# The neighbourhood attention's relative bias: loaded in the layout of its use instead of built with shift products

## The chip, the cores and the metric

The kernel runs on one core of one Trainium2 chip. Five engines work side by side, each through its own list of instructions in order: TensorE (PE, with its weight loads as PEld), VectorE (DVE), ScalarE (ACT), GpSimd (POOL) and SyncE (SP). SP and ACT also issue the DMA transfers; a DMA instruction stands in the engine's list like any other, so what follows it waits until it is issued. The metric is the time of one execution on the device in microseconds (us), as the median of several runs.

## The reference, cut to what matters

The program is two network blocks of two layers each over 256 tokens of width 1024, in float32: recurrent and block attention with a dense and a mixed-of-experts feed-forward network, then a second block on a latent stream x and a context stream. The part that changes is the neighbourhood attention in the second block. Its 256 queries are 4 grid rows of 64 columns, it has 8 heads of width 64, and a query sees the 16 columns around its own in all 4 rows, plus 256 context keys, under one softmax. A learned bias is added to the latent scores, by the distance in rows and in columns:

```python
in_win = (col[None, :] >= cs[:, None]) & (col[None, :] < cs[:, None] + kw)
dc_idx = jnp.clip(col[None, :] - col[:, None], -(kw - 1), kw - 1) + (NA_WIN_COLS - 1)
rpb_cols = rpb.astype(jnp.float32)[:, :, dc_idx]
...
    dr_idx = rs + jnp.arange(kh) - r + (NA_WIN_ROWS - 1)
    bias = jnp.take(rpb_cols, dr_idx, axis=1)
    bias = jnp.where(in_win[None, None], bias, NEG_INF)
    bias = bias.transpose(0, 2, 1, 3).reshape(h, GRID_W, kh * GRID_W)
    s_lat = jnp.einsum('bqhd,bkhd->bhqk', q_row, k_band).astype(jnp.float32) * scale + bias
```

The table `rpb` has 8 heads x 15 row distances x 31 column distances.

## The kernel before, in words

Every large product is made of weight tiles of 128 x 1024 floats. `wload` (line 295) loads one from memory into a raw tile `wraw` on SP's queue (line 305), splits it into a high part `whi` on ACT (line 246, two pieces) and a low part `wlo` on DVE (line 249, two pieces), and TensorE then multiplies high x high, low x high and high x low (line 261). There are six raw tiles and four tiles each for `whi` and `wlo`, so a load waits for an older tile's split and a split for an older tile's products.

The program is written as Python generators that are interleaved: `x_chain` carries the latent stream, and `ctx_rest` the feed-forward network of the context stream, whose work is put between the latent stream's steps at rates from the table `SIDE` (line 1993). `hT1` is the context stream's normalised input, `hid` its hidden layer, `cffy` its output, `cv` its convolution and `th` its gate. A scheduler then fixes one order for each engine. `x_chain` and `ctx_rest` start when the mixture of experts is done, behind a branch (line 1277) that all engines cross: first the layer normalisation `layer_norm` (line 426, result `h`) with its two rows `ln_g` and `ln_b` loaded on ACT's queue (line 423), then `modulated` (line 1376), which scales `h` into `xscr` and transposes it on TensorE (line 281).

`even_x` (line 1759) is the latent stream's mixer: the projections, the recurrent heads `mlstm`, their output stage `mlstm_out` (line 1709, working on `ktok`, transposed on TensorE into `yxh` and `yxl`), and then the attention. Between these two it builds the bias in two tiles `bias0` and `bias1` of 128 queries x 8 heads x 256 keys. It loads constants `consts_n` (a shift matrix and the window mask) and the table `rpb` with four DMAs (line 1775), each of 31 partitions x 8 heads x 4 floats, that is 248 pieces of 16 bytes. For each of the 64 key columns a product with a shifted slice of the matrix (line 1781) puts the right column distance on each query partition; each product is 64 x 64. It has two instructions on TensorE, so there are 128. After every eight columns VectorE adds the mask and writes the two bias tiles (line 1785, 16 additions). `attend` (line 1461) then adds the bias to the scores (line 1802, tile `S`). The loads depend on nothing computed, so the scheduler has put them right behind the branch, ahead of the first weight splits on ACT.

Of the kernel before, what the change touches and what calls it, by code (L numbers as in the profile page):

```python
# [12 lines left out]
ALU = mybir.AluOpType  # L13
# [3 lines left out]
P = 128  # L17
# [7 lines left out]
NEG = -1e30  # L25
# [33 lines left out]
def shape_consts():  # L59

    i = np.arange(P)
    parts = []

    def add(name, m):
        m = np.asarray(m, np.float32)
        parts.append((name, m))

    r, c = i[:, None], i[None, :]
    same64 = (r // 64) == (c // 64)
    add("ident", np.eye(P))  # L70
    add("ones", np.ones((P, P)))
    add("tri_incl", r <= c)
    add("tri_rev", r >= c)
    add("tri_strict", r < c)
    add("bd_incl", same64 & (r <= c))

    s, t = r % 64, np.arange(64)[None, :]
    add("h_strict", s < t)
    add("h_incl", s <= t)
    add("h_ident", s == t)  # L80
    add("lv0T", ((s // 2) == (t // 2)) & (s < t))
    for lv in range(1, 6):
        b = 2 ** lv
        add(f"lv{lv}", ((s // (2 * b)) == (t // (2 * b))) & ((s // b) % 2 == 1) & ((t // b) % 2 == 0))
    add("up", np.where(c > r, NEG, 0.0))
    add("lo", np.where(c < r, NEG, 0.0))
    add("last", np.broadcast_to(r == P - 1, (P, P)))
    add("first", np.broadcast_to(r == 0, (P, P)))
    e = np.zeros((P, 30))
    e[:64, 14] = 1  # L90
    e[64:, 15] = 1
    add("head_e", e)
    add("iota", np.broadcast_to(c, (P, P)))
    k8 = np.arange(8)
    add("lt8", np.broadcast_to((k8[None, :] < k8[:, None]).reshape(1, 64), (P, 64)))
    col = np.arange(64)
    cs = np.clip(col - 8, 0, 48)
    win = (col[None] >= cs[:, None]) & (col[None] < cs[:, None] + 16)
    add("win", np.tile(np.where(win, 0.0, NEG), (2, 1)))
    sh = np.zeros((P, 191))  # L100
    for rr in range(2):
        for dl in range(31):
            sh[rr * 32 + dl, 78 - dl + 64 * rr] = 1
    add("shift", sh)
    pos = np.arange(T)
    half = 8
    inv = np.float32(10000.0) ** (-np.arange(half, dtype=np.float32) / np.float32(half))
    cos = np.zeros((P, T), np.float32)
    sin = np.zeros((P, T), np.float32)
    rot = np.zeros((P, 32), np.float32)  # L110
    for j in range(32):
        src = (pos // 64) if j < 16 else (pos % 64)
        ang = src.astype(np.float32) * inv[j % 8]
        for base in (0, 64):
            cos[base + j] = np.cos(ang)
            sin[base + j] = np.sin(ang)
            if j % 16 < 8:
                rot[base + j + 8, j] = -1.0
            else:
                rot[base + j - 8, j] = 1.0  # L120
    add("cos", cos)
    add("sin", sin)
    add("rot", rot)
    groups = {"consts_w": ("bd_incl", "h_strict", "h_incl", "h_ident", "lv0T", "lv1", "lv2", "lv3", "lv4", "lv5"),
              "consts_n": ("win", "shift"), "consts_m": ("cos", "sin")}
    groups["ident"] = ("ident",)
    special = {n for g in groups.values() for n in g}
    groups["consts"] = tuple(n for n, _ in parts if n not in special)
    arrs, offs = {}, {}
    by = dict(parts)  # L130
    for g, names in groups.items():
        offs[g] = {}
        o = 0
        for n in names:
            offs[g][n] = (o, by[n].shape[1])
            o += by[n].shape[1]
        arrs[g] = np.ascontiguousarray(np.concatenate([by[n] for n in names], 1))
    return arrs, offs


def pack(inputs):

    out = {}
    cols = []
    for n, k in VEC_SPECS:
        v = np.asarray(inputs[n], np.float32).reshape(k, P)
        cols.append(v.T)
    out["vecs"] = np.ascontiguousarray(np.concatenate(cols, 1))
    for n in RAW:
        out[n] = np.ascontiguousarray(np.asarray(inputs[n]))  # L150
    out["rpb"] = np.ascontiguousarray(np.asarray(inputs["ev_rpb_2"])[0].transpose(2, 0, 1))
    out.update(shape_consts()[0])
    return out


def bc(ap, axis, n):
    u = ap.unsqueeze(axis)
    shp = list(u.shape)
    shp[axis] = n
    return u.to_broadcast(shp)  # L160
# [1187 lines left out]
def small(N, name):  # L1348
    return N.tp.tile([P, 512], F32, name=name, tag="hT", bufs=4)
# [359 lines left out]
def mlstm_out(N, st, ch, E, o):  # L1709

    nc = N.nc
    hs = E["kh"][:, 1024:2048]
    og = E["qo"][:, 1024:2048]
    g = N.row_load(N.a["ev_ml_norm_g_2"][0])
    N.tt(hs, hs, og, ALU.mult)
    h3 = hs.rearrange("p (n x) -> p n x", n=8)
    mu = N.sm(8, "mu")
    nc.vector.tensor_reduce(mu, h3, axis=AX.X, op=ALU.add)
    N.ts(mu, mu, 1.0 / 128)
    N.tt(h3, h3, bc(mu, 2, 128), ALU.subtract)  # L1720
    N.act(og, hs, AF.Square)
    vr = N.sm(8, "vr")
    nc.vector.tensor_reduce(vr, og.rearrange("p (n x) -> p n x", n=8), axis=AX.X, op=ALU.add)
    rs = N.sm(8, "rs")
    N.rpow(rs, vr, 8, 1.0 / 128, 1e-6)
    N.tt(h3, h3, bc(rs, 2, 128), ALU.mult)
    h2 = hs.rearrange("p (b x) -> p b x", b=2)
    N.tt(h2, h2, bc(g[:, :512], 1, 2), ALU.mult)
    for k in range(0, 4, 2):
        p = N.ps(ch)  # L1730
        for i in range(2):
            for tb in range(2):
                N.tr(p[:, i * T + tb * P:i * T + (tb + 1) * P], h2[:, tb, (k + i) * P:(k + i + 1) * P])
        N.split(o.h[:, (4 + k) * T:(6 + k) * T], o.l[:, (4 + k) * T:(6 + k) * T], p)
# [24 lines left out]
def even_x(N, st, ch, x, S):  # L1759
    nc, a, c = N.nc, N.a, N.c  # L1760
    yield from even_proj(N, st, ch, x, S, "Ex")
    E, Ec = st["Ex"], st["Ec"]
    yield from paced(mlstm(N, st, ch, E, st["CT"], st["ms"], True), SIDE["mlstm"])
    o = N.act_slots(S["h"][0], S["h"][1], "yx")
    mlstm_out(N, st, ch, E, o)
    N.load_consts("consts_n", small(N, "consts_n"))

    bias = [N.slot(S["b"][i], f"bias{i}") for i in range(2)]
    rp = small(N, "rpb")
    nc.gpsimd.memset(rp[:, 0:64], 0.0)  # L1770
    r4 = rp[:, 0:64].rearrange("p (t h j) -> p t h j", t=2, h=8)
    for rr in range(2):
        for jt in range(2):
            s = 7 - 2 * jt - rr
            nc.scalar.dma_start(r4[rr * 32:rr * 32 + 31, jt], a["rpb"][:, :, s:s + 4])

    sh = c["shift"]
    for c0 in range(0, 64, 8):
        p = N.ps(ch)
        for i in range(8):  # L1780
            N.mm(p[:, i * 64:(i + 1) * 64], sh[:64, 63 - c0 - i:191 - c0 - i], rp[:64, 0:64], True, True)
        for jt in range(2):
            src = p.rearrange("p (c t x) -> p t x c", c=8, t=2)[:, jt]
            dst = bias[jt].rearrange("p (x c) -> p x c", c=64)[:, :, c0:c0 + 8]
            N.tt(dst, src, bc(c["win"][:, c0:c0 + 8], 1, 32), ALU.add)
        yield SIDE["bias"]
    qo, kv, kvc = E["qo"], E["kv"], Ec["kv"]

    def score(pr, hh, qt, p):
        q = slice(hh * 64, hh * 64 + 64)  # L1790
        l = qo[q, pr * T + qt * P:pr * T + (qt + 1) * P]
        N.mm(p[:, 0:T], l, kv[q, pr * T:(pr + 1) * T], True, True)
        N.mm(p[:, T:2 * T], l, kvc[q, pr * T:(pr + 1) * T], True, True)

    def vsrc(pr, hh, b):
        t = kv if b < 2 else kvc
        o_ = 1024 + (b % 2) * 512 + (2 * pr + hh) * 64
        return t[:, o_:o_ + 64]

    def biased(pr, hh, qt, p, S_):  # L1800
        h = 2 * pr + hh
        N.stt(S_[:, 0:T], p[:, 0:T], 0.125, bias[qt][:, h * T:(h + 1) * T], ALU.mult, ALU.add)
        N.act(S_[:, T:2 * T], p[:, T:2 * T], AF.Copy, scale=0.125)
    yield from paced(attend(N, ch, o, 4, 4, score, vsrc, 0.125, biased, ch2=1 - ch), SIDE["na"])
    st["yx_act"] = o
# [187 lines left out]
SIDE = dict(moba_in=0, moba=1, moba_out=0, start=5, mlstm=1.25, bias=0.5, na=0.5, res0=3, end0=5, mla=1.5)  # L1993
# [37 lines left out]
def paced(g, n):  # L2031
    for _ in g:
        yield n
# [49 lines left out]
```

## Time and profile before

| | us |
|---|---|
| median of 3 runs | 2904.94 |
| lowest and highest run | 2902.77, 2906.64 |
| profiled execution, its own time | 2898.41 |
| span from its first to its last instruction | 2896.6 |
| TensorE busy in the span | 2786.5 |
| VectorE busy | 2248.3 |
| ScalarE busy | 1772.5 |
| shift products busy, 128 instructions | 16.1 |
| bias additions busy, 16 instructions | 6.0 |

The 1.8 us between the profiled execution's time and its span lie around the span. Instructions of one engine run in the order of its list; a row that says "[20.93 <-ACT whi L246]" means that the engine stood idle for 20.93 us until ACT's instruction of line 246 on the tile `whi` had ended. The profiled execution is 6.5 us below the median of the runs.

### The profile page before, as it was taken

The numbers are of one execution on the slowest core, as the hardware profiler recorded it, in microseconds if no ns is written. First come the engines' busy times: TensorE is split into PE (matmuls) and PEld (weight loads), VectorE is DVE, ScalarE is ACT, GpSimd is POOL, SyncE is SP. The second block draws the span as 40 slices with busy tenths as digits, with TensorE's granted clock in tenths as the row PEclk, the third lists the DMA queues.
The fourth block names the chain that finished last, engine by engine and source line by source line (L and its number), as shares of the span: only waits on it lengthen the run. The fifth ranks groups of instructions, "written<-read, shape, count | busy, mean of one in ns | idle before, by whom it ended". The sixth has DMA issues, their size and how long they took to land. (4 is left out here: it accounts for less than half of the span.)

```text
span 2896.6 us, 50253 instructions
## 1 busy us (share of the span) xinstructions
PE 2786.5 (96%) x18484; PEld 2289.8 (79%) x18484; DVE 2248.3 (78%) x4422; ACT 1772.5 (61%) x3601; POOL 67.1 (2%) x88
## 2 busy tenths in 40 slices
PE   8999899999999999999999999979999999999898
PEld 8677589897767787777778777768887899877898
DVE  7356485687588999999999999976777786876777
ACT  5223364444567878778788777855445665666655
POOL 0011100000000000000000000000000000000000
PEclk9999999999999999999999999989989999999999
DMA  7444666544449999999999999955432465521463
GB/s 247 154 148 157 215 191 183 175 135 146 132 139 335 362 327 354 352 350 337 348 362 327 358 345 350 361 189 168 142 113 85 131 190 182 157 76 52 140 188 124
DMA packets 356260, 639.22 MB, mean 221 GB/s; under 512 B 25733, under 2 KB 152965, under 8 KB 356006
## 3 DMA queue, kind: packets, MB, share of 16 engines
q1 hardware_dynamic: 348768, 625.58, 64.1%
q10 hardware_dynamic: 7238, 10.35, 1.1%
q8 instruction: 147, 2.41, 0.3%
q14 instruction: 107, 0.88, 0.1%
HBM read 634.81 MB, written 1.05 MB: 220 GB/s over the span
## 5 line engine op out<-in xcount | busy, mean ns | idle before, releaser
L249 DVE TENSOR_TENSOR wlo<-wraw,whi 128x512 fp32r<-128x512 f32 (+1 forms) x2181 | 1375.8, 683 | 269.6 <-ACT whi L246 209.0
L246 ACT ACTIVATE whi<-wraw 128x512 fp32r<-128x512 f32 (+1 forms) x2181 | 1214.4, 621 | 448.9 <-PE ps L261 331.7
L261 PE MATMUL ps<-whi,xg 128*128 128x512 f32 x1792 | 498.8, 397 | 2.0 <-ACT whi L246 2.0
L261 PEld LDWEIGHTS ps<-whi,xg 128*128 128x128 f32 x1792 | 327.2, 188 | 86.5 <-ACT whi L246 25.8
L261 PE MATMUL ps<-wlo,xg 128*128 128x512 f32 x896 | 295.7, 398 | 0.0
L261 PE MATMUL ps<-whi,hT 128*128 128x512 f32 x896 | 260.1, 400 | 0.0
L261 PE MATMUL ps<-hT0h,whi 128*128 128x256 f32 (+2 forms) x872 | 216.9, 286 | 3.8 <-ACT whi L246 3.3
L261 PE MATMUL ps<-hT0l,whi 128*128 128x256 f32 (+2 forms) x872 | 216.8, 286 | 0.1
L261 PEld LDWEIGHTS ps<-wlo,xg 128*128 128x128 f32 x896 | 168.1, 188 | 56.2 <-DVE wlo L249 20.8
L261 PE MATMUL ps<-whi,hid 128*128 128x512 f32 x704 | 191.9, 408 | 9.6 <-DVE cv L258 3.7
L261 PEld LDWEIGHTS ps<-whi,hT 128*128 128x128 f32 x896 | 164.4, 188 | 32.7
L261 PEld LDWEIGHTS ps<-hT0h,whi 128*128 128x128 f32 (+2 forms) x872 | 168.5, 194 | 4.9 <-ACT whi L246 3.5
L261 PEld LDWEIGHTS ps<-hT0l,whi 128*128 128x128 f32 (+2 forms) x872 | 168.5, 193 | 0.9 <-DVE hT0l L249 0.4
L261 PE MATMUL ps<-wlo,hT 128*128 128x512 f32 x448 | 168.4, 417 | 0.0
L261 PEld LDWEIGHTS ps<-whi,hid 128*128 128x128 f32 x704 | 132.5, 192 | 44.9 <-issue 12.6
L261 PE MATMUL ps<-hT1h,whi 128*128 128x256 f32 (+1 forms) x504 | 132.7, 298 | 20.9 <-ACT whi L246 20.9
L258 DVE SCALAR_TENSOR_TENSOR cv<-ps,vecs,cv 128x255 f32<-128x255 f32 x264 | 124.7, 478 | 14.0 <-ACT cv L246 12.6
L261 PE MATMUL ps<-hT1l,whi 128*128 128x256 f32 (+1 forms) x504 | 130.3, 293 | 0.0
L261 PE MATMUL ps<-hT0h,wlo 128*128 128x256 f32 (+2 forms) x872 | 124.5, 285 | 1.1 <-DVE wlo L249 1.0
L261 PEld LDWEIGHTS ps<-hT1h,whi 128*128 128x128 f32 (+1 forms) x504 | 100.2, 199 | 23.5 <-ACT whi L246 21.4
L261 PEld LDWEIGHTS ps<-hT0h,wlo 128*128 128x128 f32 (+2 forms) x872 | 113.6, 192 | 2.2 <-DVE wlo L249 1.7
L261 PEld LDWEIGHTS ps<-wlo,hT 128*128 128x128 f32 x448 | 84.2, 188 | 28.6 <-DVE wlo L249 11.1
(531 smaller groups left out, 4557.1 us busy)
## 6 DMA issues: line engine op xcount, KB each, us to landing
wraw<-moe_w_down SPq DMA_DIRECT2D x224, 512.0 KB, 5.6
wraw<-moe_w_gate SPq DMA_DIRECT2D x222, 512.0 KB, 5.2
wraw<-moe_w_up SPq DMA_DIRECT2D x222, 512.0 KB, 5.5
wraw<-ffn_w_up SPq DMA_DIRECT2D x154, 512.0 KB, 3.8
wraw<-ada_w SPq DMA_DIRECT2D x96, 512.0 KB, 4.6
wraw<-ffn_w_down SPq DMA_DIRECT2D x88, 512.0 KB, 3.9
wraw<-ev_w_in SPq DMA_DIRECT2D x56, 512.0 KB, 3.8
wraw<-rwkv_w_rkv SPq DMA_DIRECT2D x24, 512.0 KB, 6.0
```

Source lines behind the costliest of these rows:

```text
L246: self.nc.scalar.activation(out, in_, f, **kw)
L249: (eng or self.nc.vector).tensor_tensor(out, x, y, op=op)
L258: (eng or self.nc.vector).scalar_tensor_tensor(out, x, s, y, op0=op0, op1=op1)
L261: self.nc.tensor.matmul(out, l, r, start=start, stop=stop)
```

## The change

The bias comes ready from memory: `rpb` is now laid out as 64 query columns x 8 heads x 15 row distances x 64 key columns with the mask in it, 1.97 MB, and each bias tile is written by two DMAs on ACT's queue, one for each half of its partitions. The constants, the table's small loads, the products and the additions are gone. The tiles `bias0` and `bias1` lie in slots that the recurrent heads use before, so the four loads stand behind the recurrent heads in the program, ahead of `mlstm_out`. The rates are kept: what eight steps of 0.5 gave the context stream is now given in one step.

```diff
-    add("win", np.tile(np.where(win, 0.0, NEG), (2, 1)))
...
-    add("shift", sh)
...
+def rpb_layout(rpb):
+    q, k = np.arange(64)[:, None], np.arange(64)[None, :]
+    first = np.clip(q - 8, 0, 48)
+    win = (k >= first) & (k < first + 16)
+    t = rpb[:, :, np.clip(15 + k - q, 0, 30)]
+    return np.ascontiguousarray(np.where(win, t, np.float32(NEG)).transpose(2, 0, 1, 3))
...
     yield from paced(mlstm(N, st, ch, E, st["CT"], st["ms"], True), SIDE["mlstm"])
+
+    bias = [N.slot(S["b"][i], f"bias{i}") for i in range(2)]
+    for jt in range(2):
+        for rr in range(2):
+            r0 = 7 - 2 * jt - rr
+            nc.scalar.dma_start(bias[jt][rr * 64:rr * 64 + 64].rearrange("p (h x) -> p h x", h=8),
+                                a["rpb"][:, :, r0:r0 + 4].rearrange("q h r k -> q h (r k)"))
     o = N.act_slots(S["h"][0], S["h"][1], "yx")
     mlstm_out(N, st, ch, E, o)
-    N.load_consts("consts_n", small(N, "consts_n"))
-
-    bias = [N.slot(S["b"][i], f"bias{i}") for i in range(2)]
-    rp = small(N, "rpb")
-    nc.gpsimd.memset(rp[:, 0:64], 0.0)
-    r4 = rp[:, 0:64].rearrange("p (t h j) -> p t h j", t=2, h=8)
-    for rr in range(2):
-        for jt in range(2):
-            s = 7 - 2 * jt - rr
-            nc.scalar.dma_start(r4[rr * 32:rr * 32 + 31, jt], a["rpb"][:, :, s:s + 4])
-
-    sh = c["shift"]
-    for c0 in range(0, 64, 8):
-        p = N.ps(ch)
-        for i in range(8):
-            N.mm(p[:, i * 64:(i + 1) * 64], sh[:64, 63 - c0 - i:191 - c0 - i], rp[:64, 0:64], True, True)
-        for jt in range(2):
-            src = p.rearrange("p (c t x) -> p t x c", c=8, t=2)[:, jt]
-            dst = bias[jt].rearrange("p (x c) -> p x c", c=64)[:, :, c0:c0 + 8]
-            N.tt(dst, src, bc(c["win"][:, c0:c0 + 8], 1, 32), ALU.add)
-        yield SIDE["bias"]
+    yield 8 * SIDE["bias"]
```

The order of instructions moves at three places. The first is ACT's list behind the branch, where the second block starts. Before:

```order
L423 DMA row<-ln_g 128x1024
L423 DMA row<-ln_b 128x1024
L221 DMA consts_n<-consts_n 128x255
L1775 DMA rpb<-rpb 31x8x4 x3
L246 ACTIVATE whi<-wraw 128x512 x2
L1775 DMA rpb<-rpb 31x8x4
L246 ACTIVATE whi<-wraw 128x512 x3
```

With the change:

```order
L424 DMA row<-ln_g 128x1024
L424 DMA row<-ln_b 128x1024
L247 ACTIVATE whi<-wraw 128x512 x5
L247 ACTIVATE sq,ss<-h_4135 128x512 x2
L247 ACTIVATE whi<-wraw 128x512 x3
```

The five DMAs that stood ahead of or between the first weight splits are gone; the lines of VectorE at this place keep their order.

The second place is ACT's list at the end of the recurrent heads (`dw`, `den`, `num` and `ktok` are theirs; `cv`, `th` and `hid` the context stream's). Before:

```order
L246 ACTIVATE dw<-dw,ee_32162 128x128 x4
L246 ACTIVATE cv<-ps,vecs 128x256
L246 ACTIVATE den<-num 128x2
L246 ACTIVATE cv<-ps,vecs 128x256
L246 ACTIVATE den<-num 128x2
L246 ACTIVATE whi<-wraw 128x512 x2
L246 ACTIVATE cv<-ps,vecs 128x256 x2
L246 ACTIVATE th<-cv 128x512
```

With the change:

```order
L247 ACTIVATE dw<-dw,ee_32162 128x128 x4
L1770 DMA bias_33763<-rpb 64x8x256
L247 ACTIVATE den<-num 128x2 x2
L247 ACTIVATE cv<-ps,vecs 128x256 x2
L1770 DMA bias_33763<-rpb 64x8x256
L247 ACTIVATE cv<-ps,vecs 128x256 x2
L1770 DMA bias_33764<-rpb 64x8x256
L247 ACTIVATE th<-cv 128x512
L1770 DMA bias_33764<-rpb 64x8x256
L247 ACTIVATE hid_33318<-th 128x512
```

The four new loads stand between `dw` and `hid`, and `den` now goes ahead of `cv` (VectorE's list does the same).

The third place is TensorE's list at `mlstm_out`. Before:

```order
L261 MATMUL ps<-whi,hid_33318 128x512 x10
L261 MATMUL ps<-wlo,hid_33318 128x512 x4
L261 MATMUL ps<-whi,hid_33318 128x512 x6
L281 MATMUL ps<-ident,ktok_31804 128x128 x8
L261 MATMUL ps<-rpb,consts_n 128x64 x8
L261 MATMUL ps<-wlo,hid_33318 128x512 x4
L261 MATMUL ps<-rpb,consts_n 128x64 x16
L261 MATMUL ps<-hT1h,whi 128x256
```

With the change:

```order
L262 MATMUL ps<-whi,hid_33318 128x512 x6
L262 MATMUL ps<-wlo,hid_33318 128x512 x4
L262 MATMUL ps<-hT1h,whi 128x256
L262 MATMUL ps<-hT1l,whi 128x256
...
L282 MATMUL ps<-ident,ktok_31804 128x128 x8
L262 MATMUL ps<-hT1h,whi 128x256
```

The shift products, of which three more groups stood between the `hT1` products further down, are gone, and eight `hT1` products now precede the transposes of `ktok`.

## Rows read from the trace of the kernel before

**Rows 1.** The page, busy time by engine and granted TensorE clock in 40 slices.

```profile
PE 2786.5 (96%) x18484; PEld 2289.8 (79%) x18484; DVE 2248.3 (78%) x4422; ACT 1772.5 (61%) x3601; POOL 67.1 (2%) x88
...
PEclk9999999999999999999999999989989999999999
```

**Rows 2.** Stretches behind the branch: length, busy time (count) by engine, PEclk, DMA share, GB/s.

```profile
1908.00:1910.00 2.00, 0.00 (x0) 0.00 (x0) 0.23 (x1) 0.00 (x0) 0.00 (x0) 0.50 1.00 334
...
1918.00:1920.00 2.00, 0.00 (x0) 0.00 (x0) 0.00 (x0) 0.00 (x0) 0.00 (x0) 0.50 0.32 105
```

**Rows 3.** Instructions in order of time, ACT behind the branch: start, length, instruction, [idle before].

```profile
1906.54 1.25 ACTq L1775 DMA_DIRECT2D rpb<-rpb  x1
1907.83 5.09 ACTq L1775 DMA_DIRECT2D rpb<-rpb  x1
1912.95 7.55 ACTq L1775 DMA_DIRECT2D rpb<-rpb  x1
1920.55 0.63 ACT L246 ACTIVATE whi<-wraw 128x512 fp32r<-128x512 f32 x1 [22.17 <-DMA wraw<-ffn_w_up]
```

**Rows 4.** Instructions in order of time, TensorE around the branch.

```profile
1899.91 0.39 PE L261 MATMUL ps<-yl,moe_work 128*128 128x512 f32 x1
...
1921.23 0.58 PE L261 MATMUL ps<-hT1h,whi 128*128 128x256 f32 x1 [20.93 <-ACT whi L246]
```

**Rows 5.** SP behind the branch: issues in order of time; landing of line 305's four from 1903 to 1912.

```profile
1903.99 0.40 SPq L305 DMA_DIRECT2D wraw<-ffn_w_up  x1
...
1910.66 0.37 SPq L305 DMA_DIRECT2D wraw<-ffn_w_up  x1
...
DMA to landing us min/median/max: 5.7/6.6/9.2
```

**Rows 6.** Instructions in order of time, DVE and TensorE: normalisation, scaling and transposes.

```profile
1909.77 2.48 DVE L258 SCALAR_TENSOR_TENSOR h<-moe_acc,mv,row 128x1024 f32<-128x1024 f32 x2 [2.35 <-DMA row<-ln_g]
1912.41 2.74 DVE L258 SCALAR_TENSOR_TENSOR h<-h,rs,row 128x512 f32<-128x512 f32 x4 [0.15 <-DMA row<-ln_b]
...
1927.26 0.75 DVE L253 TENSOR_SCALAR xscr<-h,rs 128x1024 f32<-128x1024 f32 x1 [0.43 <-POOL rs L292]
...
1928.95 0.60 PE L281 MATMUL ps<-ident,xscr 128*128 128x128 f32 x4
```

**Rows 7.** Groups by line from 2130 to 2260 us: count, busy, mean ns, idle before.

```profile
L261 PE MATMUL ps<-rpb,consts_n 64*128 64x64 f32 x128 | 16.1, 282 | 0.0
...
L249 DVE TENSOR_TENSOR bias<-ps,consts_n 128x256 f32<-128x256 f32 x16 | 6.0, 419 | 7.5 <-PE ps L261 7.5
```

**Rows 8.** Stretches in which the bias is built, columns as in rows 2.

```profile
2155.00:2195.00 40.00, 40.00 (x279) 38.83 (x280) 19.95 (x40) 11.11 (x21) 0.00 (x0) 0.83 0.30 93
...
2162.60:2166.10 3.50, 3.50 (x19) 3.50 (x18) 2.42 (x5) 0.00 (x0) 0.00 (x0) 0.51 0.27 67
...
2172.90:2176.30 3.40, 3.40 (x17) 3.40 (x17) 2.62 (x6) 0.56 (x1) 0.00 (x0) 0.50 0.21 45
...
2184.80:2190.00 5.20, 5.20 (x25) 5.18 (x25) 3.10 (x7) 0.56 (x1) 0.00 (x0) 0.50 0.32 101
2190.00:2193.00 3.00, 3.00 (x26) 2.87 (x25) 0.57 (x1) 1.75 (x4) 0.00 (x0) 1.00 0.03 8
```

**Rows 9.** Issue of weight loads (ns min/median/max), size and landing; DMA traffic from 2136 to 2146.

```profile
L305 SPq DMA_DIRECT2D wraw<-ffn_w_up x154: 367/368/992, 394.2 to 2835.3; - x154
...
wraw<-ffn_w_up SPq DMA_DIRECT2D x154, 512.0 KB, 3.8
...
DMA packets 41, 0.04 MB, mean 4 GB/s; under 512 B 1, under 2 KB 41, under 8 KB 41
```

**Rows 10.** In order of time around the recurrent heads' end; last, the tile S (first, last start).

```profile
2138.48 1.80 PE L261 MATMUL ps<-whi,hid 128*128 128x512 f32 x4 [3.46 <-DVE cv L258]
...
2151.90 1.22 DVE L249 TENSOR_TENSOR ktok<-ktok,row 128x1024 f32<-128x1024 f32 x1
...
L258 DVE SCALAR_TENSOR_TENSOR S<-ps,bias x16: 409/416/422, 2196.3 to 2249.3; 128x256 f32<-128x256 f32 x16
```

More of the change, by code (lines that the diff above doesn't have):

```diff
@@ L95, in shape_consts @@
     add("lt8", np.broadcast_to((k8[None, :] < k8[:, None]).reshape(1, 64), (P, 64)))
-    col = np.arange(64)
-    cs = np.clip(col - 8, 0, 48)
-    win = (col[None] >= cs[:, None]) & (col[None] < cs[:, None] + 16)
-    add("win", np.tile(np.where(win, 0.0, NEG), (2, 1)))
-    sh = np.zeros((P, 191))
-    for rr in range(2):
-        for dl in range(31):
-            sh[rr * 32 + dl, 78 - dl + 64 * rr] = 1
-    add("shift", sh)
     pos = np.arange(T)
@@ L124, in shape_consts @@
     groups = {"consts_w": ("bd_incl", "h_strict", "h_incl", "h_ident", "lv0T", "lv1", "lv2", "lv3", "lv4", "lv5"),
-              "consts_n": ("win", "shift"), "consts_m": ("cos", "sin")}
+              "consts_m": ("cos", "sin")}
     groups["ident"] = ("ident",)
@@ L150, in pack @@
         out[n] = np.ascontiguousarray(np.asarray(inputs[n]))
-    out["rpb"] = np.ascontiguousarray(np.asarray(inputs["ev_rpb_2"])[0].transpose(2, 0, 1))
+    out["rpb"] = rpb_layout(np.asarray(inputs["ev_rpb_2"], np.float32)[0])
     out.update(shape_consts()[0])
@@ L1763, in even_x @@
     yield from paced(mlstm(N, st, ch, E, st["CT"], st["ms"], True), SIDE["mlstm"])
+    bias = [N.slot(S["b"][i], f"bias{i}") for i in range(2)]
[4 more added lines that the diff above has]
+                                a["rpb"][:, :, r0:r0 + 4].rearrange("q h r k -> q h (r k)"))
     o = N.act_slots(S["h"][0], S["h"][1], "yx")
     mlstm_out(N, st, ch, E, o)
-    N.load_consts("consts_n", small(N, "consts_n"))
-    bias = [N.slot(S["b"][i], f"bias{i}") for i in range(2)]
-    rp = small(N, "rpb")
-    nc.gpsimd.memset(rp[:, 0:64], 0.0)
-    r4 = rp[:, 0:64].rearrange("p (t h j) -> p t h j", t=2, h=8)
-    for rr in range(2):
-        for jt in range(2):
-            s = 7 - 2 * jt - rr
-            nc.scalar.dma_start(r4[rr * 32:rr * 32 + 31, jt], a["rpb"][:, :, s:s + 4])
-    sh = c["shift"]
-    for c0 in range(0, 64, 8):
-        p = N.ps(ch)
-        for i in range(8):
-            N.mm(p[:, i * 64:(i + 1) * 64], sh[:64, 63 - c0 - i:191 - c0 - i], rp[:64, 0:64], True, True)
-        for jt in range(2):
-            src = p.rearrange("p (c t x) -> p t x c", c=8, t=2)[:, jt]
-            dst = bias[jt].rearrange("p (x c) -> p x c", c=64)[:, :, c0:c0 + 8]
-            N.tt(dst, src, bc(c["win"][:, c0:c0 + 8], 1, 32), ALU.add)
-        yield SIDE["bias"]
+    yield 8 * SIDE["bias"]
     qo, kv, kvc = E["qo"], E["kv"], Ec["kv"]
```

## The prediction

> **What bounds the kernel now.** I read the page first. TensorE is busy for 2786.5 of 2896.6 us and its granted clock is full in nearly all slices [rows 1], so the end is set by TensorE's work and by the few places where it stands still or runs at half clock. Then I looked, in the stretches and in order of time, at the two places that the change touches.
>
> The first is the start of the second block. TensorE ends the experts near 1900.3 and starts again at 1921.23, after 20.93 us of idleness that ended with ACT's first weight split [rows 4]. ACT could not start that split before 1920.55, because three small loads of the bias table stood ahead of it and held its queue for 1.25, 5.09 and 7.55 us, the last until 1920.50 [rows 3]. The reader should not take the releaser that the row names, a weight load, for the cause: the first weight load was issued at 1903.99, and the landings there took 5.7 to 9.2 us [rows 5], so it was in between 1909.7 and 1913.2. The fourth load, issued at 1910.66, goes by the built order through the same semaphore lane as the first and waits for it, so the first was in by then. The small loads fall into a stretch in which the DMA engines are fully taken, while no compute engine does much [rows 2].
>
> The second is the building of the bias, 2155 to 2195. TensorE is busy for all 40 us, VectorE for half, the DMA engines for 0.30 [rows 8]: TensorE sets the pace. In it lie 128 instructions of shift products, 16.1 us [rows 7]. The granted clock is only 0.83: behind each of the three longer groups of shift products there is a stretch of `hT1` products at 1.2 instead of 2.4 GHz, 3.5, 3.4 and 5.2 us long, though TensorE never idles; the same `hT1` products run at full clock in between [rows 8].
>
> **The change part by part.**
>
> *Shift products.* 128 instructions leave the engine that sets the pace: 16.1 us [rows 7]. The groups overlap their neighbours slightly, so I take 16. The 16 additions, 6.0 us on VectorE, go too, but VectorE waited 7.5 us for those products and is half idle there: nothing.
>
> *Half clock.* 12.1 us at half clock cost 6.0 us of TensorE's time. The stretches begin at the groups of 64 x 64 products and nowhere else in the 40 us, so I let them go with the products: 6. The lower end is 0, the upper 6.
>
> *Lost cover.* The shift products gave TensorE work while the next tiles were made ready. Without them it comes to the transposes of `ktok` and to the low parts of the `hT1` weights sooner; VectorE finishes `ktok` at 2153.1 [rows 10], and behind that it must evacuate the transposes before it splits those weights. Also, VectorE's `cv` now stand behind `den` and `ktok`, for which TensorE already waits 3.46 us [rows 10]: two multiplications and two additions of 0.41 us and one of 1.2 us come ahead, about 3 us, of which the later wait for `hid` takes up most. I charge 3, between 0 and 7.
>
> *Small loads at the start.* Five DMAs leave ACT's queue (and one memset of 0.15 us leaves POOL, where nothing waits). ACT's first split then starts when the first weight tile is in, near 1910.4, and TensorE 10 us earlier. It can't keep all of it. The normalisation on VectorE ends at 1915.1 as before, since it waits for its rows [rows 6]; only behind it can VectorE make the low parts and `xscr`, and TensorE's order has the transposes of `xscr` behind about 40 `hT1` products. Before, `xscr` started 6.7 us after ACT came free [rows 3, 6]. Counting VectorE's and ACT's lists from 1915.1, with 0.68 us a low part, 0.62 a split and 0.9 for POOL's root, it starts at 1919.5 in place of 1927.26, and its second half likewise, so 7.8 us earlier. I take 8, between 4 (a first tile landing at 1913.2, a second later still) and 10. Two weight loads that waited for lanes of `ln_g` and `consts_n` are free of that wait by the new order.
>
> *New loads.* Four DMAs of 64 partitions x 8 pieces of 1 KB, 512 KB each. The nearest row is the `ffn_w_up` load: also 512 pieces of 1 KB, 0.37 us to issue and 3.8 us to land [rows 9]. The other end is a small `rpb` load, 7.55 us to issue while the DMA engines were full [rows 3]. At the new place they are almost empty, 0.04 MB in 10 us [rows 9], so I take 0.37 each, 1.5 us on ACT, between waits that it has there anyway: nothing on the path, since ACT's neighbours `den` and `cv` wait for VectorE and TensorE. The bias is first read near 2196.3 before [rows 10], now some 20 us after the attention's place has moved up, still about 40 us behind the issue; at 3.8 us each, in a row, the four need about 15. Behind them on ACT stand `den`, `cv` and `hid`, for which VectorE and TensorE wait, so a slow issue would cost in full. SP's loads that share lanes with them wait for their landing only when the DMAs are otherwise idle.
>
> *Sum.* 16 + 6 - 3 + 8 = 27 us. Against the profiled execution, 2898.4 becomes 2871.4; the median of the runs is 6.5 above that execution, so I forecast 2904.9 - 27 = 2878. A difference of 0.2%, about 5.8 us, is roughly what a measurement of this kernel can tell from no change. Everything behind 2260 keeps its order and only moves.
>
> **The rivals.**
>
> *The clock stays low.* The three stretches could be an echo of the idleness before 2150, and move rather than go. For it: TensorE was busy throughout, so its idleness does not explain them. Against it: they follow the groups, at three places, and end each time before the next. Then 21 us remain: 2884. The Trainium skill (TensorE: Matmul & The Clock Gate, "What's actually happening") says that the clock goes by how busy the engine has been and that idleness lowers it; by that alone, products that keep TensorE busy would not lower it and this rival would hold. The trace goes against so simple a reading: busy 40.00 of 40.00 us at a clock of 0.83 [rows 8].
>
> *The start gains nothing.* The first split is bound by its weights or the normalisation, and the lead is used up in waits at `xscr`. For it: the normalisation ends at 1915.1 whatever ACT does. Against it: from 1915.1 to 1920.5 all engines stand still but for DMA [rows 2]. Then 19 us remain: 2886. With both rivals together, 13 us remain: 2892.
>
> *Hidden, no change.* The weights' path, not TensorE, holds 2155 to 2195. Against it: VectorE is busy for 20, ACT for 11 of 40 us, DMA for 0.30 [rows 8]. This would leave the 8 us of the start or less: 2897 to 2905.
>
> *Slower.* The new loads behave as the old ones did and hold ACT at issue, now between `dw` and `hid`, where TensorE and VectorE wait for ACT. At 30 ns a piece (7.55 us for 248 pieces) 512 pieces take 15.6 us, four of them 62; less the 27 gained, 35 us slower: 2940. It decides from an issue of about 7 us on (27 / 4). For it: the same queue, more pieces. Against it: empty DMA engines and the 0.37 us of equally cut loads.
>
> **How the numbers follow.** The forecast, 2870 to 2882: 0.60. No gain at the start, 2883 to 2889: 0.13. The clock stays low, 2881 to 2887: 0.12. Both, or more cover lost than I charge, 2888 to 2899: 0.08. Hidden: 0.03. Slower: 0.04. The forecast's own bounds are 22 + 10 = 32 us, 2873, and 16 - 7 + 4 = 13 us, 2892; with the runs' scatter of 4 us the range is 2870 to 2893. Faster 0.93, same 0.03, slower 0.04.
>
> **What would show it.** In the profile after: ACT's first split near 1910 and TensorE's first `hT1` product near 1911; the transposes of `xscr` near 1921; four bias loads issued in under 0.5 us each near 2127; no stretch at 1.2 GHz in the `hT1` products behind `mlstm_out`; the first `S` near 2169 where it was at 2196.3. I am wrong if a bias load's issue takes microseconds, if TensorE's idleness around `ktok` grows by more than 5 us, or if the first split still starts near 1920.

## The result, and the profile after

The changed kernel takes 0.9884 of the time of the one before, with a 95% interval from 0.9871 to 0.9897: of 2904.94 us that is 33.7 us less (29.9 to 37.5). A second set of runs of the same kernel gave 0.9881 (0.9859 to 0.9902). The forecast was 27 us less, with 12 to 35 as its range. The page of the profiled execution (span 2867.5 us, before 2896.6), in the rows that answer to [rows 1]:

```profile
PE 2763.4 (96%) x18356; PEld 2268.0 (79%) x18356; DVE 2243.2 (78%) x4406; ACT 1773.8 (62%) x3601; POOL 67.0 (2%) x87
...
PEclk9999999999999999999999999999999999999999
```

TensorE is busy for 23.1 us less, and the two slices that showed a lower clock before are full.

**The start.** Instructions in order of time (start, length, instruction, idle before it), ACT, VectorE and TensorE behind the branch, to be held against [rows 3, 4, 6]; the last row, from the end of the recurrent heads, against [rows 10]:

```profile
1904.62 1.48 ACTq L424 DMA_DIRECT2D row<-ln_b  x1
1909.88 1.15 ACT L247 ACTIVATE whi<-wraw 128x512 fp32r<-128x512 f32 x2 [11.42 <-DMA wraw<-ffn_w_up]
1910.57 0.58 PE L262 MATMUL ps<-hT1h,whi 128*128 128x256 f32 x1 [10.21 <-ACT whi L247]
...
1919.67 0.75 DVE L254 TENSOR_SCALAR xscr<-h,rs 128x1024 f32<-128x1024 f32 x1 [0.43 <-POOL rs L293]
1920.57 0.63 PE L282 MATMUL ps<-ident,xscr 128*128 128x128 f32 x4 [0.16 <-DVE xscr L254]
...
2133.03 3.75 PE L262 MATMUL ps<-whi,hid 128*128 128x512 f32 x8 [6.48 <-DVE cv L259]
```

ACT splits the first weight tile when it lands, 10.7 us earlier than before; `xscr` starts at 1919.67 where the forecast had 1919.5, and its transposes follow 8.4 us earlier than before. The rest of the lead is used up in waits, as worked out.

**The bias.** By line and tile: the four bias loads' issue times (ns, minimum/median/maximum; first to last start) and their landing, the transposes of `ktok`, the additions into `S`. They answer to [rows 9, 10].

```profile
L1770 ACTq DMA_DIRECT2D bias<-rpb x4: 541/547/599, 2125.4 to 2133.9; - x4
...
DMA to landing us min/median/max: 5.0/5.6/7.0
...
L282 PE MATMUL ps<-ident,ktok x8: 272/273/300, 2145.0 to 2145.8; 128*128 128x128 f32 x8
...
L259 DVE SCALAR_TENSOR_TENSOR S<-ps,bias x16: 414/416/419, 2163.9 to 2221.7; 128x256 f32<-128x256 f32 x16
```

The first `S` is at 2163.9, 32.4 us earlier than before, though the idleness ahead of `hid` (last row of the fence before) has grown from 3.46 to 6.48 us. Stretches of the same profile (length, busy time and count of TensorE, its weight loads, VectorE, ACT and GpSimd, granted clock, DMA share, GB/s):

```profile
1976.00:1980.00 4.00, 3.88 (x12) 3.26 (x13) 0.99 (x7) 2.21 (x4) 0.00 (x0) 0.57 0.71 223
2129.00:2136.00 7.00, 2.97 (x7) 2.42 (x8) 6.97 (x13) 1.65 (x3) 0.00 (x0) 0.56 0.94 183
2146.00:2162.00 16.00, 16.00 (x135) 16.00 (x135) 13.89 (x26) 8.48 (x17) 0.00 (x0) 1.00 0.73 233
2188.40:2198.00 9.60, 9.60 (x23) 6.17 (x22) 4.31 (x12) 3.23 (x8) 0.00 (x0) 0.50 0.07 27
```

The third row is the stretch in which the bias was built: the clock is full, where [rows 8] show 0.83. The last row is new in this profile: inside the attention TensorE runs at 1.2 GHz for 9.6 us, with the instructions that ran at full clock in the profile of before. The first addition of the bias to `S` is 32.4 us earlier, the last only 27.6: this stretch took 4.8 us back.

To compare many profiles, the span is cut at five places that every kernel has: SP's first issue behind the branch, the first transpose of `xscr`, the last product of `VC` with `mlqk` (the recurrent heads' end, ahead of the idleness before `hid`), the first and the last addition of the bias to `S`. All lengths are differences of starts, in us; the kernels below the first four rows are the experiments.

| profile of | branch to `xscr` | to `VC` | to first `S` | to last `S` | to the end | span |
|---|---|---|---|---|---|---|
| before | 25.0 | 204.6 | 62.7 | 53.0 | 647.3 | 2896.6 |
| before, second | 24.5 | 204.2 | 59.7 | 57.6 | 645.6 | 2894.8 |
| changed | 16.6 | 204.5 | 38.8 | 57.8 | 645.8 | 2867.5 |
| changed, second | 17.0 | 204.9 | 38.8 | 53.2 | 647.3 | 2867.4 |
| loads of 31 put back | 24.8 | 204.7 | 38.8 | 53.2 | 647.4 | 2874.0 |
| loads of 32 put back | 17.6 | 202.3 | 38.8 | 53.2 | 647.1 | 2864.0 |
| 64-row products put back | 16.0 | 202.4 | 61.2 | 53.2 | 644.7 | 2885.4 |
| 128-row products | 17.3 | 202.4 | 52.6 | 53.2 | 647.3 | 2877.4 |
| products as of hT1 | 17.7 | 202.4 | 54.0 | 53.2 | 645.9 | 2875.8 |
| bias loads on SP | 16.5 | 204.4 | 41.7 | 53.0 | 644.6 | 2863.0 |
| before, loads of 32 | 17.2 | 204.8 | 62.8 | 53.0 | 647.3 | 2892.2 |

### The profile page after: what moved, and what is told of

It is laid out like the page before. It is cut to its first block, busy times and chain, and to the rows that moved or that the text cites. A ratio compares the mean times of both kernels' runs of the same rounds, so it can differ in the third digit from the quotient of the medians.

```text
span 2867.5 us, 49977 instructions
## 1 busy us (share of the span) xinstructions
PE 2763.4 (96%) x18356; PEld 2268.0 (79%) x18356; DVE 2243.2 (78%) x4406; ACT 1773.8 (62%) x3601; POOL 67.0 (2%) x87
## 5 line engine op out<-in xcount | busy, mean ns | idle before, releaser
L262 PE MATMUL ps<-hT1h,whi 128*128 128x256 f32 (+1 forms) x504 | 127.7, 290 | 12.2 <-ACT whi L247 11.6
```

Source lines behind the costliest of these rows:

```text
L262: self.nc.tensor.matmul(out, l, r, start=start, stop=stop)
```

## The experiments

### The small loads alone, with 31 and with 32 partitions

Into the changed kernel, behind `mlstm_out`; the built order puts them ahead of ACT's first weight splits, as before:

```diff
+    cn, rp = small(N, "cn"), small(N, "rpd")
+    nc.scalar.dma_start(cn[:, :255], a["consts"][:, :255])
+    r4 = rp[:, 0:64].rearrange("p (t h j) -> p t h j", t=2, h=8)
+    for rr in range(2):
+        for jt in range(2):
+            s = 7 - 2 * jt - rr
+            nc.scalar.dma_start(r4[rr * 32:rr * 32 + 31, jt], a["rpb"][0:31, :, s, 0:4])
     yield 8 * SIDE["bias"]
```

> The changed kernel with the five small loads put back ahead of ACT's first weight splits (four of 31 partitions x 8 x 4 floats, one of 128 x 255), into tiles that nothing reads; no shift products. Forecast's theory: ACT's queue is held as before, the first split starts near 1920 us instead of 1909.9, the transposes of xscr 8 us later, and the kernel takes about 8 us more than the changed one (2867.5 us of span in its profile), so about 25 us less than before, ratio near 0.991. Rival (the start gains nothing, the 8 us come from elsewhere): as the changed kernel, ratio 0.988. Rival (the loads are only slow because of their place in the kernel before, not by themselves): issues under 1 us, as the changed kernel.

The second run differs in two numbers, 32 for 31.

> As the run with the small loads put back, but each of the four has 32 partitions instead of 31, so 256 pieces of 16 bytes instead of 248. If the pieces and the busy DMA engines hold ACT's queue, the issues take as long as with 31 (1.25 to 7.55 us) and the kernel takes about 8 us more than the changed one. If it is the odd number of partitions, which leaves a load to a single DMA engine, the issues take under 1 us each, the first split starts near 1911, and the time is that of the changed kernel within 2 us.

Measured: 0.9919 (0.9903 to 0.9934) with 31, 23.5 us less than before; 0.9897 (0.9881 to 0.9913) with 32, 29.9 us less. ACT behind the branch and TensorE's first product in order of time, with 31 partitions:

```profile
1906.82 0.39 ACTq L1775 DMA_DIRECT2D cn<-consts  x1
1907.31 14.30 ACTq L1780 DMA_DIRECT2D rpd<-rpb  x3
1921.65 0.63 ACT L247 ACTIVATE whi<-wraw 128x512 fp32r<-128x512 f32 x1 [22.10 <-DMA wraw<-ffn_w_up]
...
1922.33 0.58 PE L262 MATMUL ps<-hT1h,whi 128*128 128x256 f32 x1 [20.87 <-ACT whi L247]
```

And with 32:

```profile
1907.29 2.02 ACTq L1780 DMA_DIRECT2D rpd<-rpb  x3
1911.44 1.15 ACT L247 ACTIVATE whi<-wraw 128x512 fp32r<-128x512 f32 x2 [12.09 <-DMA wraw<-ffn_w_up]
1912.12 0.58 PE L262 MATMUL ps<-hT1h,whi 128*128 128x256 f32 x1 [10.84 <-ACT whi L247]
```

The three loads hold ACT for 14.30 us with 31 partitions and for 2.02 us with 32, in the same place, with the DMA engines just as full (a share of 1.01 and 1.02 from 1908 to 1910), and with more pieces. So the stall is no price of small pieces; it is a price of the number 31. Nor were the DMA engines as a whole what was short: in the kernel before, the third load held ACT until 1920.50, while their share had fallen to 0.32 [rows 2, 3]. The Trainium skill (DMA: Bandwidth & Descriptors, "Why a DMA increments its semaphore by 16 and not by 1") says that a transfer is spread over the largest number of DMA engines, at most 16, that divides the slowest dimension of both its sides: one engine for 31, 16 for 32. By that rule all 248 pieces of a load queue up at one engine that is busy with weights; the two runs agree with it. No view here shows the single DMA engines, so the queue itself was not seen.

### The same in the kernel before

```diff
-    out["rpb"] = np.ascontiguousarray(np.asarray(inputs["ev_rpb_2"])[0].transpose(2, 0, 1))
+    out["rpb"] = np.pad(np.asarray(inputs["ev_rpb_2"])[0].transpose(2, 0, 1), ((0, 1), (0, 0), (0, 0)))
...
-            nc.scalar.dma_start(r4[rr * 32:rr * 32 + 31, jt], a["rpb"][:, :, s:s + 4])
+            nc.scalar.dma_start(r4[rr * 32:rr * 32 + 32, jt], a["rpb"][:, :, s:s + 4])
```

> The kernel before with one thing changed: the table is padded by a row of zeros, and its four small loads have 32 partitions instead of 31. All orders are those of before; the shift products stay. If the start's share of the change comes from the 31 partitions alone, the first split starts near 1911.5 instead of 1920.6 (against the branch 1 us earlier or later), the transposes of xscr come 7 us earlier, and the kernel takes 6 to 8 us less than before, ratio 0.997 to 0.998. If the lead is used up behind the start, the ratio is 1.000.

Measured: 0.9976 (0.9964 to 0.9988), 7.0 us less than before. The start, in order of time:

```profile
1907.21 15.21 SPq L305 DMA_DIRECT2D wraw<-ffn_w_up  x8
...
1909.76 2.10 ACTq L1775 DMA_DIRECT2D rpb<-rpb  x3
1913.12 1.15 ACT L246 ACTIVATE whi<-wraw 128x512 fp32r<-128x512 f32 x2 [11.48 <-DMA wraw<-ffn_w_up]
...
1924.37 0.60 PE L281 MATMUL ps<-ident,xscr 128*128 128x128 f32 x4
```

From the branch to `xscr` it takes 17.2 us instead of 25.0; every later stretch is that of before within 0.2 us. One row of zeros in a table of 15 KB gives the whole share of the start.

### A bias load in the full stretch

```diff
+    for i in (12, 6):
+        t = N.slot(i, "spare")
+        for rr in range(2):
+            nc.scalar.dma_start(t[rr * 64:rr * 64 + 64].rearrange("p (h x) -> p h x", h=8),
+                                a["rpb"][:, :, 0:4].rearrange("q h r k -> q h (r k)"))
     yield from even_proj(N, st, ch, x, S, "Ex")
```

> The changed kernel with four more loads of the bias loads' shape (64 partitions x 8 pieces of 1 KB, 512 KB) into two tiles that nothing reads, the first of them ahead of ACT's first weight split, where the DMA engines are full; it tests the rival by which the bias loads hold ACT at issue. If an issue takes long because of its pieces and the full engines, the first takes over 7.5 us (512 pieces against 248) and ACT's first split starts near 1920 again. If only loads that are left to one engine do, it takes about 0.6 us, the first split is late by the 512 KB alone, 1 to 2 us, and the kernel takes at most 8 us more than the changed one (2 MB at the 334 GB/s of that stretch are 6.3 us).

Measured in one execution: only the first of the four stands ahead of the splits; the second and the third are issued further on, between splits. ACT in order of time, and last a stretch around the third:

```profile
1907.84 0.60 ACTq L1765 DMA_DIRECT2D spare<-rpb  x1
1912.36 1.15 ACT L247 ACTIVATE whi<-wraw 128x512 fp32r<-128x512 f32 x2 [12.12 <-DMA wraw<-ffn_w_up]
...
1925.25 0.56 ACTq L1765 DMA_DIRECT2D spare<-rpb  x1
1927.01 0.54 ACTq L1765 DMA_DIRECT2D spare<-rpb  x1
...
1926.00:1928.00 2.00, 2.00 (x20) 2.00 (x19) 2.00 (x4) 1.37 (x3) 0.00 (x0) 1.00 1.04 378
```

The first, 512 pieces on 64 partitions, is issued in 0.60 us, but in these 0.60 us the DMA engines were at a share of 0.50 and not yet full. The third is issued in 0.54 us with the engines at 1.04, so a full stretch does not make the issue of such a load long. The first split comes 6.25 us behind the branch (1906.11), in the changed kernel 5.92. The span is 2869.0 us, 1.5 more than that of the change. The rival "slower" took 30 ns a piece for the price of an issue; none of these four loads paid it.

### Products of three shapes in the old places

Into the changed kernel; what is put back has no loads, no additions and no reader:

```diff
-    yield 8 * SIDE["bias"]
+    for c0 in range(0, 64, 8):
+        p = N.ps(ch)
+        for i in range(8):
+            N.mm(p[:, i * 64:(i + 1) * 64], N.ident[:64, 0:128], N.ident[:64, 0:64], True, True)
+        yield SIDE["bias"]
```

> The changed kernel with 64 products of the shape of the shift products (64 x 128 by 64 x 64, 128 instructions) put back at their old places on TensorE, on the identity, with nothing that reads their result; no small loads, no additions. Forecast's theory: 16 us of TensorE and half-clock stretches behind the three longer groups, 6 us: the first tile S comes about 22 us later than 2163.9, the kernel takes about 22 us more than the changed one, ratio to before near 0.996. Rival (the low clock belongs to the place and not to the products): 16 us more, ratio near 0.994, no stretch at 1.2 GHz behind the groups or stretches elsewhere. Rival (hidden): no difference, 0.988.

> As the run with the products put back, but with 128 products of the shape of the hT1 products (128 x 128 by 128 x 256, split precision, 0.12 us each by the rows of hT1) in the same four places, so nearly the same time of TensorE, 15.4 us. If the half clock follows the 64 x 64 products, there is none here: 15 to 16 us more than the changed kernel, granted clock 1.00 in the 40 us behind the transposes of ktok. If the half clock is an echo of the idle time before, it stays: 20 to 22 us more, with stretches at 1.2 GHz in the same places.

In that run the line inside stands twice and is `N.mm(p[:, 0:T], o.hi(4)[:, 0:P], o.hi(4), True, True)`.

> As the run with 64 products of the shift products' shape put back, but with all 128 rows of TensorE in use (128 x 128 by 128 x 64) instead of 64. If the half clock comes from using half of the rows, it is gone: 16 us more than the changed kernel, ratio near 0.994. If it comes from the other thing that sets these products apart from hT1's, 64 columns of full float32 a product, it stays: 22 us more, ratio near 0.996, with stretches at 1.2 GHz behind the groups.

In that run `N.ident[:64, ...]` is `N.ident[:, ...]`. Measured: 0.9965 (0.9953 to 0.9976) with 64 rows, 0.9924 (0.9900 to 0.9949) with 128 rows, 0.9940 (0.9924 to 0.9956) with the shape of `hT1`; against the changed kernel (0.9884) these are 23.5, 11.6 and 16.3 us more. Stretches of the profile with 64 rows:

```profile
2147.00:2188.00 41.00, 41.00 (x279) 39.85 (x278) 18.65 (x34) 10.78 (x21) 0.00 (x0) 0.79 0.35 107
2151.50:2158.00 6.50, 6.50 (x31) 6.38 (x31) 1.41 (x3) 0.00 (x0) 0.00 (x0) 0.50 0.76 242
2165.00:2168.20 3.20, 3.20 (x17) 3.20 (x16) 0.26 (x1) 0.00 (x0) 0.00 (x0) 0.50 0.47 165
2175.20:2181.80 6.60, 6.60 (x32) 6.48 (x32) 2.35 (x4) 0.80 (x2) 0.00 (x0) 0.50 0.38 114
```

With 128 rows:

```profile
2144.60:2178.00 33.40, 33.40 (x288) 32.97 (x287) 19.64 (x36) 11.23 (x21) 0.00 (x0) 1.00 0.44 136
```

With the shape of `hT1`:

```profile
2143.50:2177.00 33.50, 33.48 (x277) 32.79 (x276) 19.00 (x34) 10.73 (x20) 0.00 (x0) 1.00 0.45 136
```

The products themselves with 64 and with 128 rows (busy us, mean ns, idle before):

```profile
L262 PE MATMUL ps<-ident 64*128 64x64 f32 x128 | 16.8, 291 | 0.0
L262 PE MATMUL ps<-ident 128*128 128x64 f32 x128 | 14.7, 273 | 0.0
```

To the first `S` the three take 22.4, 13.8 and 15.2 us more than the changed kernel. Only with 64 rows does the clock fall, in three stretches of 16.3 us together that begin in the last 3 us of a longer group or right behind it, although TensorE is busy for 41.00 of 41.00 us. The run with 128 rows differs from it in nothing but the operands' rows. So the half clock came with the products, and in them with the 64 rows that they use and not with the place. The rival "the clock stays low" is refuted. The Trainium skill's rule that stood beside it (TensorE: Matmul & The Clock Gate, "What's actually happening": the clock goes by how busy the engine has been) does not tell these two runs apart by their busy time, which is full in both; here the measurement decides.

### The order around `hid`

Into the changed kernel, with the same four steps of the context stream behind it:

```diff
-            nc.scalar.dma_start(bias[jt][rr * 64:rr * 64 + 64].rearrange("p (h x) -> p h x", h=8),
+            nc.sync.dma_start(bias[jt][rr * 64:rr * 64 + 64].rearrange("p (h x) -> p h x", h=8),
```

> The changed kernel with the four bias loads on SP's queue instead of ACT's. The built order of ACT and VectorE around the end of the recurrent heads is then the one of before: the cv between the den, no loads between them on ACT. Theory (the order of den and cv set the clock there): TensorE's idleness comes in three pieces again (3.5, 0.8 and 1.9 us) with products at 1.2 GHz for over 10 us, the transposes of ktok come about 4 us later than in the changed kernel, ratio near 0.990. Rival (the loads on ACT cost time): without them idleness before hid is shorter and the kernel 2 to 3 us faster, ratio near 0.987. Rival (SP is held by the wait for the slots of the recurrent heads and weights come late): TensorE waits for whi behind 2145, slower than the changed kernel by more than 5 us.

Measured: 0.9900 (0.9881 to 0.9918). TensorE's idleness in order of time:

```profile
2128.56 1.81 PE L262 MATMUL ps<-whi,hid 128*128 128x512 f32 x4 [3.46 <-DVE cv L259]
2132.00 2.05 PE L262 MATMUL ps<-whi,hid 128*128 128x512 f32 x4 [0.77 <-DVE mu L254]
2136.75 4.63 PE L262 MATMUL ps<-whi,hid 128*128 128x512 f32 x10 [1.85 <-ACT hid L247]
```

The stretch from its first product behind that idleness:

```profile
2128.60:2142.20 13.60, 10.98 (x25) 7.67 (x26) 11.32 (x18) 4.59 (x8) 2.02 (x1) 0.51 0.69 149
```

With the order of before, TensorE idles three times, 6.08 us in all, and 11.0 us of its work run at about half clock. In the changed kernel it idles once for 6.48 us, and then runs 3 us of its work at half clock (the second of its stretches above). From `VC` to the first `S` the order of before takes 41.7 us, that of the change 38.8. The theory held in the profile for the idleness, the half clock and the loss of 2.9 us, but not for the transposes of `ktok`: from `VC` to them it takes 20.5 us against 19.9, not 4 us more, and the rest is lost behind them. In the timings the two intervals overlap. The rival by which the loads on ACT cost time is not borne out, since without them the kernel is no faster. Nor is the one by which SP brings weights late: the three waits above are all the idleness that TensorE has up to the first `S`, and none is for `whi`. The order is not the whole truth either: the second profile of before has it too, and its low stretch is short.

### The two kernels again

> The changed kernel once more, unchanged, for a second profile. Its first profile has a stretch at 1.2 GHz in the attention, 2188.2 to 2198.0 us, that four runs with the same instructions there do not have (first to last addition of the bias: 57.8 us against 53.1 to 53.2). If that stretch belongs to the execution, it is gone here: 53 us, and the span is near 2863. If it belongs to the kernel, 57.8 us again. The ratio to before stays near 0.988 in both cases.

> The kernel before once more, unchanged, for a second profile and as a measure of what no change looks like: ratio 1.000 within 0.002. The half clock behind the three groups of shift products should come back (about 12 us in 2155 to 2195), and, if it belongs to the kernel, so should the one from 2138.8 to 2152.3 around ktok. If the latter is an accident of one execution, TensorE gets from its idleness before hid to the transposes of ktok in some 14 us instead of 19.

Measured: 0.9881 (0.9859 to 0.9902) for the changed kernel, 1.0005 (0.9990 to 1.0020) for the one before. The changed kernel's second profile, the additions into `S`:

```profile
L259 DVE SCALAR_TENSOR_TENSOR S<-ps,bias x16: 410/415/418, 2166.9 to 2220.1; 128x256 f32<-128x256 f32 x16
```

And a stretch of it at the place of the slow one:

```profile
2191.40:2201.00 9.60, 9.60 (x43) 6.86 (x44) 7.26 (x19) 6.25 (x15) 0.00 (x0) 1.00 0.16 51
```

Stretches of before's second profile, first behind the idleness ahead of `hid`, then behind two groups of shift products:

```profile
2136.50:2140.20 3.70, 2.90 (x6) 1.82 (x6) 3.70 (x8) 0.59 (x2) 0.00 (x0) 0.54 0.00 0
2167.80:2174.20 6.40, 6.40 (x30) 6.28 (x30) 3.10 (x7) 0.56 (x1) 0.00 (x0) 0.50 0.37 124
2181.80:2184.60 2.80, 2.80 (x15) 2.80 (x15) 2.13 (x5) 0.57 (x1) 0.00 (x0) 0.51 0.21 59
```

And its additions into `S`:

```profile
L258 DVE SCALAR_TENSOR_TENSOR S<-ps,bias x16: 412/416/420, 2191.6 to 2249.2; 128x256 f32<-128x256 f32 x16
```

The attention takes 53.2 us in the second profile of the changed kernel and 57.6 in the second one of before: its low stretch belongs to the execution, not to either kernel. The span did not become shorter by it as expected: it is 2867.4 us and not 2863, since the stretches ahead of the branch and behind the attention took 2.3 and 1.5 us more.

The long stretch around `ktok` is not there in each execution either. In the first profile of before, and in that of before with loads of 32, it is:

```profile
2138.80:2152.20 13.40, 10.77 (x25) 7.51 (x24) 11.12 (x17) 4.63 (x8) 2.02 (x1) 0.50 0.12 39
2134.40:2148.00 13.60, 10.93 (x26) 7.58 (x25) 11.32 (x17) 4.84 (x8) 2.02 (x1) 0.50 0.13 39
```

In the second profile of before, with the same order, 3.70 us are left of it. From the start of the idleness ahead of `hid` to the transposes of `ktok` that saved only 1.6 us (17.4 instead of 19.0, where 14 was expected), because TensorE then waited 1.28 us for `ktok`. The ones behind the shift products come back each time, with 9.2 us here after 12.1, and not after every group.

### Two attempts at a faster kernel

Both keep the changed kernel and try to fill the 6.48 us ahead of `hid`: two of the four context steps given ahead of `mlstm_out` (`yield 2`, then `yield 2` behind it), and `mlstm=1.375` in the table of rates.

> The changed kernel with the four steps of the context stream given in two halves, two ahead of mlstm_out and two behind it, instead of four behind it. TensorE then has hT1 products where it now idles for 6.5 us before hid, while VectorE makes ktok. Theory: the idle time and most of the half clock behind it go, 4 to 8 us less than the changed kernel, ratio 0.985 to 0.987. Rival: VectorE is full in those 6 us, the cv of the step are late either way, and the idleness only moves behind ktok: no difference, 0.988.

> The changed kernel with the context stream at 1.375 instead of 1.25 steps per step of the recurrent heads, so that the cv and hid of a step lie ahead of den and ktok. Theory: hT1 products cover the 6.5 us of idleness, 4 to 8 us less than the changed kernel, ratio 0.985 to 0.987. Rival: the context stream runs out earlier at the end, where TensorE is only 65% busy as it is (39 of 60 us from 2820), and the gain is lost there: 0.988.

Measured: 0.9874 (0.9856 to 0.9892) and 0.9948 (0.9932 to 0.9963). In the first, TensorE still waits for `cv`:

```profile
2130.09 3.75 PE L262 MATMUL ps<-whi,hid 128*128 128x512 f32 x8 [6.48 <-DVE cv L259]
```

The idleness is the same to the hundredth, since VectorE, which makes `ktok` and `cv`, sets it, and the `hT1` products that were moved forward stand behind `hid` in TensorE's list, not ahead of it; the theory fell, and the ratio can't be told from that of the change. The second is slower than the theory and the rival both said. In it the 6.48 us are gone, but with the extra context work the way from `xscr` to `VC` takes 211.9 us instead of 204.5, and behind the last `S` nothing of that comes back: 655.0 us instead of 645.8 to 647.3. The rival's 65% was a misreading: its 60 us from 2820 reach 12.5 us beyond the end, so TensorE was busy for 39 of 47.5. Why the later stages lost so much was not followed up. No version here is shown to beat the change.

## Why the prediction was right, and where its sum was off

*Start, 8 us.* Right. From the branch to `xscr` the two profiles of before take 24.7 us on average, the two of the change 16.8: 7.9. Putting the loads back took it away again (24.8), and 32 partitions gave it to the kernel before (17.2, and 7.0 us in the timings). What the prediction did not have is the cause of the long issues: it put them down to pieces in a full stretch. Its sum did not need the cause, since the loads leave whatever made them long; its rival "slower" did.

*Shift products, 16, and half clock, 6.* Right. 64-row products put back cost 22.4 us to the first `S`; the same number in shapes that keep the clock cost 13.8 and 15.2. The half clock is thus worth 7.2 to 8.6 us and the products 14 to 15; the forecast split 22 as 16 and 6. The two splits agree: the products' own rows hold 16.8 us (14.7 with 128 rows), since the clock falls before two of the longer groups end, and that leaves 5.6 us for the rows behind them.

*Lost cover, 3.* This is the step that failed. Its order is there: `cv` stand behind `ktok`, and the first wait ahead of `hid` is longer by 3.02 us. But the prediction charged 3 us for this and for low parts that are needed sooner, although it had said itself that the later wait for `hid` takes up most of the first. The later waits took up all of it, and for the second TensorE did not wait: behind `hid` it idles 0.56 us for `cffy` in one profile of the change and 0.34 for `whi` in the other, and never for `wlo`. The stretches from `VC` to the first `S`, two profiles of before and two of the change, columns as above:

```profile
2133.58:2196.31 62.73, 56.64 (x335) 50.66 (x334) 40.23 (x80) 19.19 (x36) 2.02 (x1) 0.78 0.27 85
2131.89:2191.56 59.67, 51.85 (x335) 46.52 (x334) 40.08 (x81) 19.43 (x36) 2.02 (x1) 0.89 0.29 89
2125.11:2163.88 38.77, 31.73 (x207) 28.17 (x206) 33.91 (x64) 19.05 (x36) 2.02 (x1) 0.91 0.69 189
2128.13:2166.90 38.77, 31.94 (x207) 28.42 (x206) 33.92 (x63) 19.05 (x36) 2.02 (x1) 0.91 0.69 189
```

TensorE stands still for 6.1 and 7.8 us before and for 7.0 and 6.8 with the change: the idleness has moved into one piece for the most part and has not grown. The clock behind it adds to either side: with the order of before up to 11 us of work ran at half clock, in the changed kernel 3. Against the run with 64-row products (61.2 us from `VC` to the first `S`), before has 62.7 and 59.7: the term is nothing, within 1.5 us either way, and not 3 of loss.

*Bias loads, nothing.* Right. They are issued in 0.54 to 0.60 us each, a little over the 0.37 taken, and land in 5.0 to 7.0 us, over 20 us ahead of their first use.

*Sum.* With the failed term at nothing it is 30 us instead of 27, at the lower end of the measured 29.9 to 37.5. The two pairs of profiles differ by 28.3 us: 7.9 at the start, 22.4 from `VC` to `S`, and -1.5 ahead of the branch, where the kernels are the same; the other stretches differ by 0.3 or less. The timings show 33.7 us, 5.4 more than the profiles. The profiled executions of before lie 6.5 and 3.7 us below the medians of their runs, those of the change 3.8 above and at it, so the pairs of profiles differ by less than the runs do. Low stretches that come and go (4.6 us in the attention, up to 3 around `ktok`) are large enough for this. The mean clock on record of every timed execution allows an estimate: 0.9783 over 62 of before and 0.9831 over 11 of the change make 126 and 97 us at half clock, 29 apart, where the pairs of profiles have 122 and 101; the further 8 us at half clock can cost up to 4 us. That they do so was not shown.

*The rivals.* "The start gains nothing" and "hidden" are refuted by the runs that put one part back; "slower" by issues of 0.54 to 0.60 us, even where the DMA engines are full. Of the signs named, only two were off: the issues, just above 0.5 us, and the first `S`, 2163.9 instead of 2169.

## What to carry to other kernels

A DMA that is small and slow to issue should first be looked at for its number of partitions: 31 against 32 was worth 7 us here, without any other change. Products that use half of TensorE's rows can cost more than their own time, since here the work behind them ran at half clock; a quarter of the price of the products put back (22.4 less 16.8 us) stood in rows of other instructions. When a change lengthens one wait, add up the other waits of the stretch and the clock behind them before charging it: here the later waits gave back what the first one took.

## What was not expected of the hardware

The clock of the same instructions differs from one execution to the next. In the attention the stage takes 53.0 to 53.2 us in nine of the eleven profiles of the table and 57.6 and 57.8 in two, one of each kernel, whose other profile has 53.0 and 53.2.

Between `xscr` and `VC` TensorE's products are the same in all profiles of the table, yet the stage takes 204.2 to 204.9 us or 202.3 to 202.4, nothing in between. The stretch from 1976 to 1980 has 0.57 in the profile of the change (above); the one at the same distance behind `xscr` in the run with loads of 32 has 1.00:

```profile
1978.10:1982.10 4.00, 4.00 (x21) 3.08 (x20) 2.62 (x10) 2.19 (x4) 0.00 (x0) 1.00 0.57 164
```

No kernel shows both values here, so whether this one goes by the execution or by the kernel stays open.

The Trainium skill (TensorE: Matmul & The Clock Gate, "What's actually happening") says that the clock's supervision runs free of the kernel, so that the same kernel is hit at different points from run to run; the two profiles of each kernel agree (53.0 and 57.6 us, 57.8 and 53.2). One profile's low stretch is therefore no property of a kernel until a second profile shows it too.
